# Feed-forward passes of 512 moving columns in layers 1 to 3, and smaller reorderings, in a four-layer float32 encoder trunk

## The chip, the cores and the metric

The kernel runs on one core of one Trainium2 chip. The metric is the device time of one execution in microseconds, as the median of several runs. The profile is of one further execution of the same program. TensorE is PE in its rows (its weight loads are PEld), VectorE is DVE, ScalarE is ACT, GpSimd is POOL, and SP is the queue that issues most transfers.

## What is computed

Four layers act on one sequence of 256 tokens of width 1024, in float32. Each layer has a token mixer and then a SwiGLU feed-forward of width 2816, each behind an RMSNorm and with a residual add. Layers 0 and 3 mix by attention with a forget gate, layer 1 by a diagonal state-space scan (S5), layer 2 by trailing-mean pooling.

```python
def forgetting_attention(h, w_in, b_f, w_out):
    q, k, v, f_logit = jnp.split(h @ w_in, [D_MODEL, 2 * D_MODEL, 3 * D_MODEL], axis=-1)
    log_f = jax.nn.log_sigmoid(f_logit + b_f)
    c = jnp.cumsum(log_f, axis=1).transpose(0, 2, 1)
    ...
        logits = jnp.einsum('bhqd,bhkd->bhqk', q_b, k) * scale
        logits = logits + c_b[..., :, None] - c[..., None, :]
        p = jax.nn.softmax(jnp.where(mask, logits, -jnp.inf), axis=-1)
        return jnp.einsum('bhqk,bhkd->bhqd', p, v)
    ...
    return out @ w_out

def swiglu(h, w_gate_up, w_down):
    g, u = jnp.split(h @ w_gate_up, 2, axis=-1)
    return (jax.nn.silu(g) * u) @ w_down

    for i in range(DEPTH):
        x = x + mix(rms_norm(x, mix_norm_g[i]))
        x = x + swiglu(rms_norm(x, ffn_norm_g[i]), w_gate_up[i], w_down[i])
    return rms_norm(x, final_norm_g)
```

## The kernel before

Activations lie transposed, features on the 128 partitions and the 256 tokens (`N`) along the columns. The weights come in units of 128 x 1024 float32. A unit is fetched by SP into one of four `raw` buffers; ACT then rounds it to the matmul's type (`L98`, the high part) and DVE subtracts to get the low part (`L99`), both into one of five `hl` buffers (`fetch`, `split_unit`, `unit`). Activations are split in the same way into a high and a low half, `X` in front of a projection and `H` inside the feed-forward. A product of 128 rows of the contraction is then three matmul passes of 256 columns into one PSUM bank, high by high, low by high, high by low (`term`):

```python
    def term(self, out, hl, cols, X, k, start, stop):
        self.mm(out, hl[:, 0, cols], X[:, 0, k], start, False)
        self.mm(out, hl[:, 1, cols], X[:, 0, k], False, False)
        self.mm(out, hl[:, 0, cols], X[:, 1, k], False, stop)
```

The feed-forward (`ffn`) runs 22 chunks of 128 hidden features. A chunk is two units, gate `G` and up `U`, of eight terms each, so 48 passes. `act` then takes the two banks: DVE multiplies `G` by the norm row `R` (`t`, L259), ACT applies Silu (L260), DVE multiplies with `U` (`h`, L262), ACT rounds (L178) and DVE subtracts (L179) into `H`. There are four banks with the tag `P`, two `acc` and two `tp`. The second half forms eight output tiles `d` of 22 terms each in `acc`; each is scaled by `R`, added to the residual `x` and prepared for the next norm (`settled`). A layer's feed-forward has 528 terms.

The attention (`fox`) first projects values and gates (tokens on the partitions, passes of 352, 352 and 336 columns), then `gates` computes the log-forget gate of 128 tokens at a time on ACT and DVE, PE sums it up (`sums`), DVE copies the sums out (`c`, and the transposed `nct`), and a DMA takes `nct` through memory (`nd`). `bias` on POOL reads `nd` back, spread over the partitions (`nb`), masks it and adds `c`: eight tiles of a layer, four head pairs' worth of `t` = 0 and `t` = 1. Meanwhile PE runs the q and k projections of eight head pairs, two units each. `heads` is the attention of one pair in three steps: scores on PE, then on DVE the bias and the row maximum (L402), on ACT Exp (L404), on DVE reciprocal and scaling (L407, L408); transposes of the four probability tiles on PE (L417) with copies by ACT (L419); and the product with the values, split into `oT`.

Work beside the main stream is placed by a counter: `tick` is called after a fixed number of terms (two of them in a plain projection, so four ticks a unit), and `at(n, fn)` emits `fn` n ticks later. Within a short distance the building layer may still move an instruction ahead of one that waits, so the order of each engine below is taken from the built program. Each engine executes its own list in order.

```python
            for n in (20, 25, 28):
                self.at(n, lambda steps=steps: next(steps, None))
```

Layer 0 also carries the preparation of the S5 tables (`prepare`), a long list of small DVE operations (tiles `W`, `lam`, `pa`, `pb`) that is handed out by ticks. `rstd` forms a norm row: PE sums squares (`total`), POOL raises to the power -1/2 (L228), PE spreads the row over the partitions (`spread`, L234).

Of the kernel before, what the change touches and what calls it, by code (L numbers as in the profile page):

```python
# [33 lines left out]
class Trunk:  # L34
# [128 lines left out]
    def dense(self, outs, X, ready=None):  # L163
        hls = [self.unit() for _ in outs]
        for k in range(8):
            for out, hl in zip(outs, hls):
                self.term(out, hl, slice(128 * k, 128 * k + 128), X, k, k == 0, k == 7)
                if k % 2 or len(outs) > 1 and (out is outs[1] or out is outs[-1]):
                    self.tick()

    def new_X(self, pool=None):
        return (pool or self.ap).tile([128, 2, 8, N], F32R, tag="X", name="X", bufs=1)

    def work(self, name="wk"):
        return self.ap.tile([128, N], F32, tag="wk", name=name, bufs=6)
# [5 lines left out]
    def settled(self, d, key):  # L181
# [6 lines left out]
        if key is not None and key != 2:  # L188
            g = self.gT[:, 8 * key + d:8 * key + d + 1]
            if key == 0 and d == 0:  # L190
                nc.vector.tensor_scalar(out=self.X[:, 0, d], in0=x, scalar1=g, scalar2=None, op0=ALU.mult)  # L191
            else:
                nc.scalar.activation(self.X[:, 0, d], x, AF.Identity, scale=g)  # L193
            nc.vector.scalar_tensor_tensor(out=self.X[:, 1, d], in0=x, scalar=g, in1=self.X[:, 0, d].bitcast(F32),  # L194
# [11 lines left out]
        if key is None:  # L206
            if d == 0:
                self.xg = self.ap.tile([128, 8, N], F32, tag="X", name="xg", bufs=1)
# [6 lines left out]
    def rstd(self, wait=(3, 3)):  # L215
# [34 lines left out]
    def ffn(self, l):  # L250
        nc = self.nc
        X, key = self.X, l + 1 if l + 1 < self.layers else None
        with self.tc.tile_pool(name="hidden", bufs=1, reuse_waits="tile") as hp:
            H = hp.tile([128, 2, NCH, N], F32R, name="H")
            R = self.R

            def act(i, G, U):
# [7 lines left out]
            outs = [self.bank(t)[:, 0:N] for t in ("acc", "acc", "P", "P")]  # L265
            self.dense(outs, X)
            act(0, outs[0], outs[1])
            act(1, outs[2], outs[3])
            for i in range(2, NCH):
                G, U = self.bank("P")[:, 0:N], self.bank("P")[:, 0:N]  # L270
                self.dense([G], X)
                self.dense([U], X)
                act(i, G, U)
            for d in range(8):
                o = self.bank("acc")[:, 0:N]
# [713 lines left out]
```

## Time and profile before

| | us |
|---|---|
| median of 3 runs | 1165.85 |
| lowest, highest | 1165.14, 1168.01 |
| the profiled execution | 1169.78 |
| its span (first to last instruction) | 1168.0 |
| PE busy in the span | 1133.8 |
| DVE, ACT, POOL busy | 817.0, 621.3, 130.4 |

The trace's times run from the span's start. By the stretches, layer 0's attention lies at 9 to 136 us, its feed-forward to 341; S5 at 341 to 453, feed-forward 1 to 642; pooling at 642 to 670, feed-forward 2 to 850; attention 3 at 850 to 976, feed-forward 3 to 1158. PE is busy nearly everywhere, so what counts is how many passes it runs, what one costs, and the few places where it stands. DVE is close to full only between 50 and 150 us and around 350 to 400 us. A timeline row with an xN is N instructions of one form in a row, with the time from the first start to the last end; a bracket is the idle time before the row on that engine and what ended it.

### The profile page before, as it was taken

To read this page: it belongs to the slowest core of one execution; us is meant where nothing else is said; L and a number is where in the kernel's file an instruction comes from. 1 tells how busy PE (TensorE), PEld (TensorE's weight loads), DVE (VectorE), ACT (ScalarE), POOL (GpSimd) and SP (SyncE) were. 2 spreads that over 40 slices of the span, in tenths; PEclk is the share of its full clock that TensorE was granted. 3 is DMA by queue.
4 is the path that set the end of the run, shared out by engine and by line. 5 is a ranking of instruction groups with operands and counts; after the bars stand their busy time and mean duration, and the time that the engine had idled before them with its cause. 6 is when DMAs were issued, how large, how long until landed. Compare 5 with 4: busy or idle time off the path is not lost. (4 is left out here: it accounts for less than half of the span.)

```text
span 1168.0 us, 25319 instructions
## 1 busy us (share of the span) xinstructions
PE 1133.8 (97%) x10246; PEld 1105.7 (95%) x10246; DVE 817.0 (70%) x1540; ACT 621.3 (53%) x1092; POOL 130.4 (11%) x167
## 2 busy tenths in 40 slices
PE   7899999999999999999999999999999999999996
PEld 7888899999999999999999999999999899999996
DVE  5899986888759975766555576665656767666563
ACT  5556766786852264544444554444545566444441
POOL 1287000111100000000000000000005710000000
PEclk9999999999999999999999899999999999999998
DMA  8655466788789744755566266556656644666561
GB/s 287 200 166 161 141 211 204 242 262 262 248 290 340 242 138 151 229 189 181 171 184 188 73 201 186 189 173 183 191 188 204 179 137 128 216 183 192 170 185 46
DMA packets 63285, 225.16 MB, mean 193 GB/s; under 512 B 7681, under 2 KB 8049, under 8 KB 63041
## 3 DMA queue, kind: packets, MB, share of 16 engines
q1 hardware_dynamic: 56432, 200.86, 55.0%
q0 software_dynamic: 6160, 22.00, 6.0%
q8 instruction: 80, 1.31, 0.5%
q10 hardware_dynamic: 576, 0.69, 0.2%
q14 instruction: 37, 0.30, 0.1%
HBM read 208.81 MB, written 14.71 MB: 191 GB/s over the span
## 5 line engine op out<-in xcount | busy, mean ns | idle before, releaser
L156 PE MATMUL P<-X,hl 128*128 128x256 f32 x5520 | 682.8, 284 | 2.2 <-ACT X L178 1.2
L156 PEld LDWEIGHTS P<-X,hl 128*128 128x128 f32 x5520 | 665.9, 190 | 10.8 <-issue 7.1
L98 ACT CAST hl<-raw 128x1024 fp32r<-128x1024 f32 (+3 forms) x363 | 371.7, 1027 | 394.8 <-issue 184.5
L99 DVE TENSOR_TENSOR hl<-raw,hl 128x1024 fp32r<-128x1024 f32 (+3 forms) x363 | 434.8, 1199 | 210.0 <-ACT hl L98 206.8
L156 PE MATMUL acc<-H,hl 128*128 128x256 f32 x2112 | 254.1, 281 | 0.0
L156 PEld LDWEIGHTS acc<-H,hl 128*128 128x128 f32 x2112 | 250.7, 188 | 0.8 <-issue 0.6
L156 PE MATMUL acc<-X,hl 128*128 128x256 f32 x480 | 69.4, 287 | 1.0 <-DVE u L760 0.4
L383 POOL TENSOR_SCALAR nb<-nb,c 128x128 f32<-128x128 f32 (+1 forms) x64 | 68.8, 1087 | 1.1
L156 PEld LDWEIGHTS acc<-X,hl 128*128 128x128 f32 x480 | 60.9, 188 | 3.4 <-ACT X L193 0.8
L228 POOL TENSOR_TENSOR rs<-rs,mhalf 128x2 f32<-128x2 f32 x9 | 6.5, 727 | 479.1 <-DVE rs L227 479.1
L262 DVE TENSOR_TENSOR h<-P,t 128x256 f32<-128x256 f32 x84 | 35.5, 423 | 33.6 <-PE P L156 33.4
L259 DVE TENSOR_TENSOR t<-P,R 128x256 f32<-128x256 f32 x84 | 35.5, 423 | 12.0 <-PE P L156 9.1
L404 ACT ACTIVATE pt<-pt,st 128x128 f32<-128x128 f32 (+1 forms) x64 | 28.4, 446 | 20.8 <-DVE st L402 20.7
L156 PE MATMUL P<-hl,X 128*128 128x336 f32 (+1 forms) x192 | 39.2, 324 | 0.0
L260 ACT ACTIVATE t<-t 128x256 f32<-128x256 f32 x88 | 36.4, 414 | 4.9 <-DVE t L259 4.8
L178 ACT CAST H<-h 128x256 fp32r<-128x256 f32 x88 | 35.4, 402 | 6.6 <-DVE h L262 6.6
L179 DVE TENSOR_TENSOR H<-h,H 128x256 fp32r<-128x256 f32 x88 | 36.9, 419 | 2.0 <-ACT H L178 1.9
L193 ACT ACTIVATE X<-x,gains 128x256 fp32r<-128x256 f32 x55 | 27.7, 505 | 10.8 <-DVE x L248 10.2
L202 ACT ACTIVATE s<-x 128x256 f32<-128x256 f32 x63 | 25.6, 406 | 14.4 <-DVE x L248 12.4
L156 PEld LDWEIGHTS P<-hl,X 128*128 128x128 f32 x192 | 32.7, 193 | 0.0
L156 PE MATMUL acc<-hl,X 128*128 128x352 f32 x96 | 24.6, 341 | 8.0 <-DVE X L191 7.6
L194 DVE SCALAR_TENSOR_TENSOR X<-x,gains,X 128x256 fp32r<-128x256 f32 x56 | 26.8, 480 | 5.1 <-ACT X L193 5.0
(168 smaller groups left out, 744.1 us busy)
## 6 DMA issues: line engine op xcount, KB each, us to landing
raw<-in_w_gu SPq DMA_DIRECT2D x176, 512.0 KB, 3.7
raw<-in_w_dn SPq DMA_DIRECT2D x64, 512.0 KB, 3.6
raw<-in_w_qk SPq DMA_DIRECT2D x32, 512.0 KB, 3.9
raw<-in_w_dn SPq DMA_DIRECT2D x32, 384.0 KB, 3.4
raw<-in_w_fo SPq DMA_DIRECT2D x16, 512.0 KB, 4.1
raw<-in_w_glu SPq DMA_DIRECT2D x16, 512.0 KB, 4.6
raw<-in_w_vf SPq DMA_DIRECT2D x15, 520.0 KB, 4.0
nb<-nd POOLq DMA_DIRECT2D x24, 256.0 KB, 5.2
```

Source lines behind the costliest of these rows:

```text
L98: nc.scalar.copy(hl[:, 0, s], raw[:, s])
L99: nc.vector.tensor_tensor(out=hl[:, 1, s], in0=raw[:, s], in1=hl[:, 0, s].bitcast(F32), op=ALU.subtract)
L156: self.nc.tensor.matmul(out, lhsT=lhsT, rhs=rhs, start=start, stop=stop)
L178: self.nc.scalar.copy(hi, src)
L179: self.nc.vector.tensor_tensor(out=lo, in0=src, in1=hi.bitcast(F32), op=ALU.subtract)
L193: nc.scalar.activation(self.X[:, 0, d], x, AF.Identity, scale=g)
L194: nc.vector.scalar_tensor_tensor(out=self.X[:, 1, d], in0=x, scalar=g, in1=self.X[:, 0, d].bitcast(F32), op0=ALU.mult, op1=ALU.subtract)
L259: nc.vector.tensor_tensor(out=t, in0=G, in1=R, op=ALU.mult)
L260: nc.scalar.activation(t, t, AF.Silu)
L262: nc.vector.tensor_tensor(out=h, in0=U, in1=t, op=ALU.mult)
L383: nc.gpsimd.tensor_scalar(out=nb[:, i], in0=nb[:, i], scalar1=self.c[t][:, 4 * n + i:4 * n + i + 1], scalar2=None, op0=ALU.add)
L404: nc.scalar.activation(pt, pt, AF.Exp, bias=st[:, 0:1], scale=-1.0, accum_out=st[:, 1:2])
```

## The change

1. **Wide passes.** `X` and `H` are laid out so that the high and the low half of one contraction step lie side by side (`[128, 8, 2, N]`). In the feed-forward of layers 1 to 3 a term is two passes: the high weights against both halves at once, 512 columns into a whole bank, and the low weights against the high half, 256 columns added onto the bank's second half. `fold` then adds the two halves of the bank: ACT copies the second out of PSUM, DVE adds it to the first. The last output tile (`d` = 7) of layers 1 and 3 keeps three passes. Layer 0 and all other projections keep three.
2. **Gates** of both token blocks in one set of operations, one `nct` and one `nd`, sums at tick 10 (before at 7 and 8), the first bias at 11 (before 10), the steps of `heads` at 18, 23 and 26 (before 20, 25, 28). The value copies after the first projection are in another order.
3. **Softmax scaling** of every second probability tile on ACT.
4. **Norm rows** are spread one tick later (`wait=(3, 4)`).
5. The pooling layer's second scaled band is made on ACT; S5's first two projections use `P` banks; `xg` has a buffer of its own; eight `wk` buffers.

```diff
     def term(self, out, hl, cols, X, k, start, stop):
-        self.mm(out, hl[:, 0, cols], X[:, 0, k], start, False)
-        self.mm(out, hl[:, 1, cols], X[:, 0, k], False, False)
-        self.mm(out, hl[:, 0, cols], X[:, 1, k], False, stop)
+        self.mm(out, hl[:, 0, cols], X[:, k, 0], start, False)
+        self.mm(out, hl[:, 1, cols], X[:, k, 0], False, False)
+        self.mm(out, hl[:, 0, cols], X[:, k, 1], False, stop)
...
+    def wide(self, o, hl, s, X, k, first, last):
+        self.mm(o, hl[:, 0, s], X[:, k].rearrange("p a n -> p (a n)"), first, False)
+        self.mm(o[:, N:], hl[:, 1, s], X[:, k, 0], False, last)
+
+    def fold(self, o):
+        nc = self.nc
+        lo, t = self.work("lo"), self.work("t")
+        nc.scalar.copy(lo, o[:, N:])
+        nc.vector.tensor_tensor(out=t, in0=o[:, 0:N], in1=lo, op=ALU.add)
+        return t
...
-    def rstd(self, wait=(3, 3)):
+    def rstd(self, wait=(3, 4)):
...
+            wide = l > 0
             def act(i, G, U):
-                t = self.work("t")
-                nc.vector.tensor_tensor(out=t, in0=G, in1=R, op=ALU.mult)
+                t = self.fold(G) if wide else self.work("t")
+                nc.vector.tensor_tensor(out=t, in0=t if wide else G, in1=R, op=ALU.mult)
                 nc.scalar.activation(t, t, AF.Silu)
-                h = self.work("h")
-                nc.vector.tensor_tensor(out=h, in0=U, in1=t, op=ALU.mult)
-                self.split(H[:, 0, i], H[:, 1, i], h)
+                h = self.fold(U) if wide else self.work("h")
+                nc.vector.tensor_tensor(out=h, in0=h if wide else U, in1=t, op=ALU.mult)
+                self.split(H[:, i, 0], H[:, i, 1], h)
...
+                broad = wide and not (d == 7 and key in (2, None))
+                o = self.bank("acc") if broad else self.bank("acc")[:, 0:N]
...
-            for n in (20, 25, 28):
+            for n in (18, 23, 26):
                 self.at(n, lambda steps=steps: next(steps, None))
...
-            nc.vector.tensor_copy(c, cps[:, 0:16])
-            nc.vector.tensor_copy(nct, cps[0:16, 128:256])
+            nc.vector.tensor_copy(nct, cps[0:16, 128:384])
+            nc.vector.tensor_copy(c, cps[:, 0:32])
             nc.sync.dma_start(nd, nct)
-        self.at(7 + t, sums)
+        self.at(10, sums)
...
-        for pt, st in Ps:
+        for i, (pt, st) in enumerate(Ps):
             nc.vector.reciprocal(out=st[:, 2:3], in_=st[:, 1:2])
-            nc.vector.tensor_scalar(out=pt, in0=pt, scalar1=st[:, 2:3], scalar2=None, op0=ALU.mult)
+            if i % 2:
+                nc.scalar.activation(pt, pt, AF.Identity, scale=st[:, 2:3])
+            else:
+                nc.vector.tensor_scalar(out=pt, in0=pt, scalar1=st[:, 2:3], scalar2=None, op0=ALU.mult)
...
-        nc.vector.tensor_scalar(out=sb1, in0=self.band[:, :, 144:272], scalar1=rs[:, 1:2], scalar2=None, op0=ALU.mult)
+        nc.scalar.activation(sb1, self.band[:, :, 144:272], AF.Identity, scale=rs[:, 1:2])
...
-        self.open_quad()
         for m in range(8):
             self.at(1 + 5 * m, lambda m=m: self.tables(m))
         for m in range(0, 8, 2):
-            P = [self.bank("acc")[:, 0:N] for _ in range(2)]
+            P = [self.bank("acc" if m else "P")[:, 0:N] for _ in range(2)]
             if m == 0:
                 self.dense(P, X)
+                self.open_quad()
```

Three places of the built programs follow. The number behind a name is a buffer's; `P_8953` and `P_8954` are the gate and the up bank of one chunk.

On PE, the gate and the up projection of one chunk in feed-forward 2 stood so before:

```order
L156 MATMUL P_8953<-X_8421,hl_8890 128x256 x24
L156 MATMUL P_8954<-X_8421,hl_8919 128x256 x24
```

On PE, the gate projection of a chunk of the same layer begins so now, and goes on in the same way:

```order
L156 MATMUL P_8923<-X_8052,hl_8870 128x512
L156 MATMUL P_8923<-X_8052,hl_8870 128x256
L156 MATMUL P_8923<-X_8052,hl_8870 128x512
L156 MATMUL P_8923<-X_8052,hl_8870 128x256
```

Each unit's 24 passes of 256 columns became eight pairs of 512 and 256.

On DVE, one chunk of that feed-forward before (L99 rows are weight splits; `t`, `h` and `H` are the chunk's own):

```order
L99 TENSOR_TENSOR hl_9024<-raw_8984,hl_9024 128x1024
L179 TENSOR_TENSOR H_8541<-h_8949,H_8541 128x256
L259 TENSOR_TENSOR t_9013<-P_8953,R_8537 128x256
L99 TENSOR_TENSOR hl_9053<-raw_9022,hl_9053 128x1024
L262 TENSOR_TENSOR h_9016<-P_8954,t_9013 128x256
```

On DVE, one chunk of it now:

```order
L183 TENSOR_TENSOR t_8968<-P_8923,lo_8967 128x256
L277 TENSOR_TENSOR t_8968<-t_8968,R_8168 128x256
L99 TENSOR_TENSOR hl_9005<-raw_8982,hl_9005 128x1024
L183 TENSOR_TENSOR t_8974<-P_8924,lo_8973 128x256
L280 TENSOR_TENSOR t_8974<-t_8974,t_8968 128x256
L99 TENSOR_TENSOR hl_9041<-raw_9003,hl_9041 128x1024
L194 TENSOR_TENSOR H_8172<-t_8974,H_8172 128x256
```

Two additions (L183) joined the five operations, and between any two groups of the chunk's own stands a weight split; on ACT the order is copy, weight cast, Silu, copy, weight cast, cast of `H`.

On ACT, one head pair of layer 3 before, from the last Exp on (L404 and L430 are Exp, L98 is a weight cast, L435 the scaling, L419 and L448 the copies of the transposes, L178 and L193 the cast of `oT`):

```order
L404 ACTIVATE pt_11644,st_11645<-pt_11644,st_11645 128x256
L98 CAST hl_11829<-raw_11790 128x1024
L419 COPY pT_11705<-tp_11702 128x256
L419 COPY pT_11712<-tp_11707 128x512
L98 CAST hl_11909<-raw_11827 128x1024
L178 CAST X_10986<-tp_11751 128x256
```

On ACT, one head pair of layer 3 now:

```order
L430 ACTIVATE pt_10875,st_10876<-pt_10875,st_10876 128x256
L435 ACTIVATE pt_10867<-pt_10867,st_10868 128x128
L98 CAST hl_11035<-raw_10946 128x1024
L435 ACTIVATE pt_10875<-pt_10875,st_10876 128x256
L448 COPY pT_10925<-tp_10922 128x256
L448 COPY pT_10932<-tp_10927 128x512
L98 CAST hl_11084<-raw_11033 128x1024
L193 CAST X_10233<-tp_10963 128x256
```

A weight cast now stands between the two scalings on ACT; it does so in 13 of the 16 head pairs, in the last three of layer 3 it stands behind them.

## Rows read from the trace of the kernel before

**Rows 1.** The page, part 1: span and PE's busy time, share and instructions

```profile
span 1168.0 us, 25319 instructions
PE 1133.8 (97%) x10246; PEld 1105.7 (95%) x10246; DVE 817.0 (70%) x1540; ACT 621.3 (53%) x1092; POOL 130.4 (11%) x167
```

**Rows 2.** Busy time by stretches: stretch, length, engines with counts, clock, DMA

```profile
50.00:100.00 50.00, 47.09 (x389) 43.10 (x390) 47.91 (x145) 25.86 (x60) 42.67 (x42) 0.97 0.59 172
...
750.00:800.00 50.00, 50.00 (x422) 50.00 (x422) 30.86 (x44) 23.38 (x34) 0.00 (x0) 1.00 0.58 178
```

**Rows 3.** Timeline of PE, value projection of layer 3 (start, length, instruction)

```profile
862.64 0.48 PE L156 MATMUL acc<-hl,X 128*128 128x352 f32 x2
...
871.20 0.48 PE L156 MATMUL acc<-hl,X 128*128 128x352 f32 x2
```

**Rows 4.** The page, part 5: groups, busy us and mean ns, idle before

```profile
L98 ACT CAST hl<-raw 128x1024 fp32r<-128x1024 f32 (+3 forms) x363 | 371.7, 1027 | 394.8 <-issue 184.5
L99 DVE TENSOR_TENSOR hl<-raw,hl 128x1024 fp32r<-128x1024 f32 (+3 forms) x363 | 434.8, 1199 | 210.0 <-ACT hl L98 206.8
...
L262 DVE TENSOR_TENSOR h<-P,t 128x256 f32<-128x256 f32 x84 | 35.5, 423 | 33.6 <-PE P L156 33.4
...
L260 ACT ACTIVATE t<-t 128x256 f32<-128x256 f32 x88 | 36.4, 414 | 4.9 <-DVE t L259 4.8
```

**Rows 5.** Timeline of PE where a norm row is spread

```profile
346.16 0.43 PE L234 MATMUL tp<-cst,rs 128*128 128x128 f32 x2 [0.48 <-POOL rs L228]
...
455.24 0.43 PE L234 MATMUL tp<-cst,rs 128*128 128x128 f32 x2 [0.54 <-POOL rs L228]
```

**Rows 6.** Timeline: start of S5 on PE, start of pooling on DVE

```profile
349.14 0.98 PE L156 MATMUL acc<-X,hl 128*128 128x256 f32 x6 [0.42 <-DVE u L760]
...
645.14 0.48 DVE L452 TENSOR_SCALAR sb<-band,rs 128x512 f32<-128x512 f32 x1
```

**Rows 7.** Timeline: the gate's sums on PE, copies of them on DVE

```profile
45.10 0.40 PE L156 MATMUL tp<-lf,cst 128*128 128x16 f32 x2 [1.92 <-DVE lf L356]
...
45.05 0.27 DVE L370 COPY nct<-tp 16x128 f32<-16x128 f32 x1
```

**Rows 8.** Timeline of POOL: the bias tiles of layers 0 and 3

```profile
50.05 2.59 POOL L379 DMA_DIRECT2D nb<-nd  x4 [27.13 <-DMA nd<-nct]
...
61.61 9.62 POOL L383 TENSOR_SCALAR nb<-nb,c 128x256 f32<-128x256 f32 x8
...
897.82 6.24 POOL L383 TENSOR_SCALAR nb<-nb,c 128x256 f32<-128x256 f32 x6
```

**Rows 9.** Timeline: the first head pair's softmax and transposes, layers 0 and 3

```profile
69.03 0.70 PE L417 MATMUL tp<-cst,pt 128*128 128x128 f32 x4 [0.34 <-DVE pt L408]
...
900.19 0.43 DVE L402 CUSTOM_DVE_ANT_0 pt<-acc,nb 128x256 f32<-128x256 f32 x1 [0.27 <-POOL nb L383]
...
902.41 0.44 PE L417 MATMUL tp<-cst,pt 128*128 128x128 f32 x2 [0.22 <-DVE pt L408]
```

**Rows 10.** Waits of PE, layer 0's attention: total us, times, longest

```profile
PE tp L417 <- DVE pt L408: 2.5, 4, 1.6
...
PE tp L417 <- DVE st L407: 0.8, 1, 0.8
```

**Rows 11.** Timeline of one late head pair of layer 3

```profile
956.07 0.93 PE L156 MATMUL acc<-kT,q 64*128 64x128 f32 x8
...
957.92 0.28 DVE L402 CUSTOM_DVE_ANT_0 pt<-acc,nb 128x128 f32<-128x128 f32 x1
...
959.52 0.49 ACT L404 ACTIVATE pt<-pt,st 128x256 f32<-128x256 f32 x1
...
960.05 1.05 ACT L98 CAST hl<-raw 128x1024 fp32r<-128x1024 f32 x1
...
960.57 0.82 PE L417 MATMUL tp<-cst,pt 128*128 128x128 f32 x6
```

**Rows 12.** Timeline of PE: the attention's output projection, last step

```profile
964.89 1.22 PE L156 MATMUL P<-X,hl 128*128 128x256 f32 x8 [0.60 <-ACT X L178]
```

More of the change, by code (lines that the diff above doesn't have):

```diff
@@ L253, in ffn @@
         with self.tc.tile_pool(name="hidden", bufs=1, reuse_waits="tile") as hp:
[L254 removed]
+            H = hp.tile([128, NCH, 2, N], F32R, name="H")
             R = self.R
+            wide = l > 0
+            cut = (lambda z: z) if wide else (lambda z: z[:, 0:N])
             def act(i, G, U):
[L258 to L259 removed]
+                t = self.fold(G) if wide else self.work("t")
+                nc.vector.tensor_tensor(out=t, in0=t if wide else G, in1=R, op=ALU.mult)
                 nc.scalar.activation(t, t, AF.Silu)
[L261 to L266 removed]
+                h = self.fold(U) if wide else self.work("h")
+                nc.vector.tensor_tensor(out=h, in0=h if wide else U, in1=t, op=ALU.mult)
+                self.split(H[:, i, 0], H[:, i, 1], h)
+            outs = [cut(self.bank(t)) for t in ("acc", "acc", "P", "P")]
+            self.dense(outs, X, wide)
             act(0, outs[0], outs[1])
@@ L269, in ffn @@
             for i in range(2, NCH):
-                G, U = self.bank("P")[:, 0:N], self.bank("P")[:, 0:N]
-                self.dense([G], X)
-                self.dense([U], X)
+                G, U = cut(self.bank("P")), cut(self.bank("P"))
+                self.dense([G], X, wide)
+                self.dense([U], X, wide)
                 act(i, G, U)
             for d in range(8):
-                o = self.bank("acc")[:, 0:N]
+                broad = wide and not (d == 7 and key in (2, None))
+                o = self.bank("acc") if broad else self.bank("acc")[:, 0:N]
                 for u, ks in enumerate((8, 8, 6)):
@@ L279, in ffn @@
                         f = 8 * u + k
-                        self.term(o, hl, slice(128 * k, 128 * k + 128), H, f, f == 0, f == NCH - 1)
+                        s = slice(128 * k, 128 * k + 128)
+                        (self.wide if broad else self.term)(o, hl, s, H, f, f == 0, f == NCH - 1)
                         if k % 2:
                             self.tick()
-                t = self.work("t")
-                nc.vector.tensor_tensor(out=t, in0=o, in1=R, op=ALU.mult)
+                t = self.fold(o) if broad else self.work("t")
+                nc.vector.tensor_tensor(out=t, in0=t if broad else o, in1=R, op=ALU.mult)
                 self.add(d, t)
@@ L342, in fox, with gates @@
             self.settled(d, 4 + l)
-    def gates(self, j, t, zp, r, bf):
+    def gates(self, j, zp, rs, bf):
         nc, mp = self.nc, self.mp
-        z = mp.tile([128, 4, 16], F32, tag="z", name="z", bufs=2)
-        nc.vector.scalar_tensor_tensor(out=z[:, 0], in0=zp[:, 0:16], scalar=r, in1=bf, op0=ALU.mult, op1=ALU.add)
-        lf = mp.tile([128, 16], F32, tag="lf", name="lf", bufs=2)
-        self.lf.append(lf)
+        z = mp.tile([128, 4, 32], F32, name="z")
+        for t in range(2):
+            nc.vector.scalar_tensor_tensor(out=z[:, 0, 16 * t:16 * t + 16], in0=zp[t][:, 0:16], scalar=rs[:, t:t + 1],
+                                           in1=bf, op0=ALU.mult, op1=ALU.add)
+        lf = mp.tile([128, 32], F32, name="lf")
         nc.vector.tensor_scalar(out=z[:, 1], in0=z[:, 0], scalar1=-1.0, scalar2=None, op0=ALU.mult)
@@ L857, in emit @@
         nc.scalar.activation(g.rearrange("p (j r) -> p r j", r=4), yv, AF.Gelu_apprx_tanh)
-        self.split(G[:, 0, m], G[:, 1, m], g)
+        self.split(G[:, m, 0], G[:, m, 1], g)
         self.emitted = m + 1
```

73 lines of the change are left out of this document (41 added, 32 removed).

## The prediction

> **What bounds the kernel now.** I read the page's first part, then the stretches, then the timeline at the places where PE stands. PE is busy 1133.8 of 1168.0 us [rows 1], so the time is the number of its passes times the price of one, plus a few waits. In the feed-forwards PE never stops: 50 us hold 422 passes of 256 columns [rows 2], which is 118.5 ns a pass, while DVE is busy 31 and ACT 23 of the 50. The other kind of stretch is attention in layer 0, where DVE is busy 47.9 of 50 us and PE does 389 instructions [rows 2]. There and in layer 3 PE waits for chains of small operations on other engines [rows 7, 9, 12]. So I ask of the wide passes what they take off PE, and of everything else which wait ends last.
>
> **Wide passes.** 506 of the 528 terms in layers 1 and 3 (the 22 of d = 7 stay out) and 528 in layer 2 are widened: 1540 terms. Each loses one pass and one weight load and keeps its 768 columns. A pass of 512 columns does not occur before, so its price is bounded from the nearest rows. In layer 3's value projection 54 passes of mean 346.7 columns (1040/3) lie between 862.64 and 871.20 us [rows 3], 158.5 ns each. Against 118.5 ns at 256 [rows 2] that is 40.0 ns for 90.7 columns, 0.441 ns a column, and leaves 5.6 ns for the pass itself. On this line 512 columns take 118.5 + 256 x 0.441 = 231.4 ns, and a term goes from 355.5 to 349.9 ns: 5.6 ns less. Bounds: if price is proportional to columns, 237 ns and no gain; if a column takes 1/2.4 ns (the granted clock is 1.00 of 2.4 GHz in this stretch [rows 2]) and the other 118.5 - 106.7 = 11.8 ns belong to the pass, 225.1 ns and 11.8 ns gained. I take the line, because it needs only the two widths that the trace has: 1540 x 5.6 ns = **8.6 us off**, between 0 and 18.2.
>
> The Trainium skill (TensorE: Matmul & The Clock Gate, section Back-to-back issue gap) gives N/2.4 + 2.5 ns for a warm pass in a stream, that is 109.2 ns at 256 columns. The rows show 118.5 [rows 2] and disagree by 9 ns. By that formula for both widths a term would lose just its 2.5 ns, 3.9 us in all.
>
> **What folding adds, and what hides it.** A chunk gets two ACT copies and two DVE additions of 128x256. On DVE it then has five operations of about 0.42 us [rows 4] and two weight splits of 1.2: 4.5 us. ACT has two copies, Silu and a cast at about 0.41 and two weight casts of 1.03: 3.7 us. PE needs 16 x (231.4 + 118.5) ns = 5.6 us for the chunk, so both stay under it. The waits inside the chain are covered by order: between any two steps of the chunk on DVE stands a weight split of 1.2 us, in which ACT does the 0.41 us that the next step wants. PE holds four P banks, two chunks, and five weight buffers, so one late chunk does not reach it. Cost taken: nothing; without this cover see rival 4. An output tile has 22 x 0.35 = 7.7 us of PE over some 5 us of DVE. The extra 0.8 us until x is updated falls before work that comes later: the tile d = 7 in front of pooling and the end is not folded, and in front of layer 3 the attention needs it only with its eighth unit.
>
> **Norm rows.** Four times PE stands before L234, 0.48 to 0.54 us, for POOL's power ([rows 5] has two of them, the others are at 672.7 and 978.2). One tick more is two terms in these projections, 0.7 us, which covers it: **2.0 us off**.
>
> **S5 and pooling.** The wait of 0.42 us for the eviction of an acc bank [rows 6] goes when the first two tiles use P: 0.4 off. The second band no longer queues its 0.48 us behind the first on DVE [rows 6]: 0.4 off. xg, wk and the layouts cost and bring nothing that the rows show, since PE waits for none of them.
>
> **Attention.** Here moves compete with each other, and I go by what ends last.
>
> First head pair. Scores need q and k; the softmax needs nb, which hangs on the chain gate sums, nct, nd, POOL. Before, PE stood 1.92 us for the second block's gate alone in layer 0 [rows 7], and it still had to stand again at the first transposes [rows 9]: in layer 3 DVE's fourth score tile waited for POOL and began at 900.19, and the last transposes at 902.41. So the nb chain is what ends last, and time saved ahead of it is lost in the wait for it. The change does not shorten that chain. The nct copy of both blocks comes when the second one came, one weight split (1.2 us) further down DVE's list: layer 0 before had the first nct at 45.05 and POOL's reads, freed by nd, from 50.05 [rows 7, 8]. I take +0.5 us in layer 3 (bounds 0 and 1.2) and 0 in layer 0, where POOL's operations cost 1.2 us each against 1.04 in layer 3 [rows 8] and a waiting DVE gives some back. Behind the fourth tile the last scaling now runs on ACT: 0.5 us after the tile's start Exp can begin, it and its read take 0.7 (0.49 the Exp [rows 11]), a scaling 0.4 (as Silu [rows 4]), the weight cast that stands ahead 1.05, a scaling 0.4. That ends 3.05 + 0.5 us after 900.2, about 903.7 against 902.4. And the pair starts two ticks earlier, so that 12 passes, 1.4 us, are still to do then. Layer 3: 1.3 + 1.4 = 2.7 us lost; layer 0, whose DVE was as late before, 1.4 us lost.
>
> Later pairs. Before, the scores fell on a unit's end, so the weight split released there stood ahead of the softmax: scores began at 956.07, the softmax only at 957.92, and PE's transposes followed at 960.57 without a gap [rows 11]. Two ticks earlier, the scores fall into the middle of a unit, the weight cast and split of the unit before are done, and the softmax can begin some 1.1 us earlier. ACT's last Exp then ends near 958.9, its first scaling at 959.4, the cast of 1.05 us [rows 11] at 960.4, its second scaling at 960.8; PE wants that tile four transposes (0.4 us) behind the first, at 961.0. So the extra cast is just covered: nothing gained or lost, and if the cover failed each of 13 pairs would pay (rival 3). In layer 0 PE waits at transposes for 2.5 + 0.8 us, 1.6 and 0.3 of it in the first pair [rows 9, 10]; the other 1.4 should go with 16 scalings off DVE. The last wait, 0.60 us for oT before the last step of the output projection, stands in both layers ([rows 12] has one, the other is at 136.2) and goes, since that step comes two ticks earlier: 1.2 off. Attention in sum: 2.7 + 1.4 - 1.4 - 1.2 = **1.5 us on**, with 3 us either way.
>
> **Sum.** -8.6 - 2.0 - 0.4 - 0.4 + 1.5 = -9.9 us. Against the profiled execution (1169.78, span 1168.0 and 1.8 around it) that gives 1159.9; this execution is 3.9 us above the median, and as the terms are differences I apply them to the median: 1165.85 - 9.9 = **1156 us**.
>
> **Rivals.**
> 1. *Only columns count.* A pass has no price of its own and 512 cost 237 ns. For it: 118.5 to 158.5 ns for 256 to 346.7 columns is nearly proportional (0.463 and 0.457 ns a column). Against it: the line through them still leaves 5.6 ns. Gives 1165.85 - 1.3 = 1164.6, the case too that the change does not do what it says. The Trainium skill's formula named above would give 1160.7 here.
> 2. *The surplus over the clock belongs to the pass.* 11.8 ns gained a term, 18.2 us: 1165.85 - 19.5 = 1146.4. For it: PE's clock is full [rows 2]. Against it: the surplus is larger for 346.7 columns (14.1 ns).
> 3. *The cast between the scalings shows.* If the softmax does not begin earlier, the last scaling ends 1.0 us after PE wants it, in 13 pairs: +13, so 1169, within the band of no change. For it: DVE is full in layer 0. Against it: the weight units' ends have moved, by the order of the program.
> 4. *Folding binds the feed-forward* (slower). DVE's 4.5 us a chunk fit into 5.6 only if its waits for ACT stay under 1.1. If both copies, Silu and the cast of H were all waited for, 3 x 0.41 + 0.40 us come on top: 6.2 us against 5.7 before. 66 chunks lose 33 us, the gain of 5.9 in these chunks goes, and the time is 1165.85 - 9.9 + 5.9 + 33 = 1195. It decides from 1.1 us of such waits. For it: DVE works in order and folding adds two hops. Against it: the splits between the steps, and DVE at 31 of 50 us now.
>
> **How the numbers follow.** A measurement of this kernel can tell about 0.3%, 3.5 us, from no change; faster means under 1162.4. Chances: the forecast 0.54 (own range 1151 to 1160), rival 1 0.16 (half of it above 1162.4, since 0 to 3 ns a term lie in it), rival 2 0.13, rival 3 0.09, rival 4 0.05, and 0.03 for a slower time from something unseen. Faster 0.54 + 0.13 + 0.08 = 0.75; same 0.08 + 0.09 = 0.17, slower 0.08. The range takes in the forecast, rival 1 and most of rival 2: 1145 to 1164.5.
>
> **What would show it.** In the feed-forward stretches of layers 1 to 3, 50 us should hold about 143 pairs of passes (50/0.35) with PE full; 140.6 would be rival 1, 145.5 rival 2. If PE shows idle time there that DVE ends, rival 4 holds. L234 should have no wait but in pooling and at the end. The first transposes of layers 0 and 3 should show a longer wait than before, ended by ACT's scaling, and the later ones none; waits of 1 us there would be rival 3. The gate sums should have none. I would be wrong above all if a 512-column pass costs other than 231 ns, since 1540 of them multiply the error.

## The result, and the profile after

| | before | changed |
|---|---|---|
| median of 5 runs, us | 1167.73 | 1157.62 |
| lowest, highest | 1165.14, 1169.14 | 1155.12, 1161.29 |
| span of the profiled execution | 1168.0 | 1155.8 |
| PE rows in it | 10246 | 8706 |

The ratio of the means is 0.9923, 95% interval 0.9897 to 0.995. That is 9.0 us less by the means, 10.1 by the medians and 12.2 by the two profiled spans. The forecast was 1156, worked out from a median of 1165.85 before; the five runs here have 1167.73.

The page of the changed kernel, part 1, answers to [rows 1]: 1540 passes fewer, and DVE and ACT with 52 and 62 us more.

```profile
span 1155.8 us, 22388 instructions
PE 1119.3 (97%) x8706; PEld 1027.9 (89%) x8706; DVE 868.6 (75%) x1647; ACT 683.7 (59%) x1273; POOL 121.5 (11%) x167
```

Stretches of feed-forwards 2 and 3 in the changed kernel (columns as in [rows 2], whose second row they answer to):

```profile
675.00:800.00 125.00, 125.00 (x723) 110.24 (x722) 100.52 (x160) 77.04 (x134) 0.00 (x0) 1.00 0.62 193
980.00:1090.00 110.00, 110.00 (x636) 97.00 (x635) 89.55 (x146) 68.96 (x122) 0.00 (x0) 1.00 0.61 195
```

PE never stops, DVE and ACT have room. 723 passes are 361.5 pairs: 345.8 ns a term, where 349.9 were forecast. (Both stretches lie mostly in the gate and up half of a feed-forward.)

PE's waits in the changed kernel, whole program (us in total, times, longest):

```profile
PE tp L446 <- DVE pt L437: 6.3, 3, 5.6
PE tp L249 <- POOL rs L243: 3.8, 6, 1.1
PE tp L446 <- DVE st L433: 2.4, 2, 2.0
PE tp L446 <- ACT pt L435: 2.0, 4, 0.7
PE P L156 <- DVE t L183: 2.0, 2, 1.0
PE P L156 <- ACT y L501: 1.3, 1, 1.3
```

The L446 rows are the transposes of attention, L249 the norm rows, and L183, the fold, is new: PE waits for it twice.

Lengths of stages are read below from the first pass that spreads a norm row to the last pass of that layer. Feed-forwards 1, 2 and 3 took 185.7, 177.6 and 179.3 us before and 183.5, 173.2 and 175.3 after; everything up to the end of layer 0 took 341.0 and 340.9.

### The profile page after: what moved, and what is told of

It is laid out like the page before. It is cut to its first block, busy times and chain, and to the rows that moved or that the text cites. A ratio compares the mean times of both kernels' runs of the same rounds, so it can differ in the third digit from the quotient of the medians.

```text
span 1155.8 us, 22388 instructions
## 1 busy us (share of the span) xinstructions
PE 1119.3 (97%) x8706; PEld 1027.9 (89%) x8706; DVE 868.6 (75%) x1647; ACT 683.7 (59%) x1273; POOL 121.5 (11%) x167
## 5 line engine op out<-in xcount | busy, mean ns | idle before, releaser
L156 PE MATMUL P<-X,hl 128*128 128x256 f32 (+1 forms) x4560 | 678.1, 308 | 3.4 <-DVE t L183 2.0
L156 PEld LDWEIGHTS P<-X,hl 128*128 128x128 f32 x4560 | 618.2, 190 | 52.7 <-issue 6.9
L99 DVE TENSOR_TENSOR hl<-raw,hl 128x1024 fp32r<-128x1024 f32 (+3 forms) x363 | 434.7, 1199 | 143.0 <-ACT hl L98 134.9
L98 ACT CAST hl<-raw 128x1024 fp32r<-128x1024 f32 (+3 forms) x363 | 372.3, 1028 | 162.3 <-PE acc L156 75.5
L156 PE MATMUL acc<-H,hl 128*128 128x512 f32 (+1 forms) x1628 | 251.1, 315 | 0.0
L156 PEld LDWEIGHTS acc<-H,hl 128*128 128x128 f32 x1628 | 226.6, 188 | 21.1 <-issue 0.6
L182 ACT COPY lo<-P 128x256 f32<-128x256 f32 x126 | 46.8, 372 | 107.8 <-PE P L156 107.8
L183 DVE TENSOR_TENSOR t<-P,lo 128x256 f32<-128x256 f32 x126 | 53.2, 424 | 44.4 <-ACT lo L182 44.3
L156 PE MATMUL acc<-X,hl 128*128 128x256 f32 (+1 forms) x384 | 61.3, 300 | 0.1
L156 PEld LDWEIGHTS acc<-X,hl 128*128 128x128 f32 x384 | 50.5, 188 | 3.7 <-DVE X L194 0.3
L430 ACT ACTIVATE pt<-pt,st 128x128 f32<-128x128 f32 (+1 forms) x64 | 28.6, 448 | 24.5 <-DVE st L428 24.3
L280 DVE TENSOR_TENSOR t<-t 128x256 f32<-128x256 f32 x66 | 28.0, 424 | 1.9
L277 DVE TENSOR_TENSOR t<-t,R 128x256 f32<-128x256 f32 x66 | 28.0, 424 | 1.7
```

Source lines behind the costliest of these rows:

```text
L98: nc.scalar.copy(hl[:, 0, s], raw[:, s])
L99: nc.vector.tensor_tensor(out=hl[:, 1, s], in0=raw[:, s], in1=hl[:, 0, s].bitcast(F32), op=ALU.subtract)
L156: self.nc.tensor.matmul(out, lhsT=lhsT, rhs=rhs, start=start, stop=stop)
L182: nc.scalar.copy(lo, o[:, N:])
L183: nc.vector.tensor_tensor(out=t, in0=o[:, 0:N], in1=lo, op=ALU.add)
L277: nc.vector.tensor_tensor(out=t, in0=t if wide else G, in1=R, op=ALU.mult)
```

## The experiments

All times are medians, each kernel compared with runs of the kernel before on the same chip; ratios are of the means, with their 95% interval. The kernel before had medians of 1167.86 us beside narrow, swap, spread7 and first28, 1168.52 beside nbchain, dvescale, heads20 and wide0, and 1169.57 beside before_wide, best and best_w0. So a difference of 2 us from the changed kernel's 1157.62 says little, and where two intervals overlap the rows have to decide. Unless it is said otherwise, a kernel is the changed one with the edit shown.

### Wide passes off, and alone

**narrow**

```diff
-            wide = l > 0
+            wide = False
```

> The changed kernel with three passes of 256 columns again in every feed-forward; the rest of the change stays. My theory: a wide term saves 9.6 ns (start to start 229.8 + 117.0 ns against 3 x 118.8), 1540 terms 14.8 us, of which three waits at the start of each wide feed-forward (1.2, 1.4, 1.1 us, for a bank that the fold still reads) take 3.7 back. So this kernel should take 11 us more than the changed one, 1168 to 1169 us, its 512-column rows gone, the three waits gone and 50 us of feed-forward 2 again holding some 422 passes. Rival, the line of the prediction (5.6 ns a term, 8.6 us): only 5 us more, 1162.5, and the rest of the gain would have to come from the attention and the pooling.

1168.07 us, ratio to before 0.9997 (0.9985 to 1.0009). All of the gain hangs on the wide passes, and the rest of the change is worth nothing that can be measured. The same stretches in narrow:

```profile
675.00:800.00 125.00, 125.00 (x1053) 125.00 (x1053) 79.50 (x109) 59.14 (x88) 0.00 (x0) 1.00 0.63 191
980.00:1090.00 110.00, 110.00 (x926) 110.00 (x925) 73.22 (x104) 55.59 (x83) 0.00 (x0) 1.00 0.62 194
```

1053 passes in 125 us are 356.1 ns a term, so a wide term saves 10.3 ns here. The starts of the single passes between 680 and 775 us say the same and say where: a pass of 256 columns takes 119.0 ns from its start to the next one's in narrow; in the changed kernel one of 512 takes 229.9, and the one of 256 behind it 117.0. That is 10.1 ns a term.

The price holds in the gate and up half of a feed-forward (1056 of the 1540 terms). In the half that forms the output tiles the wide terms save less: from the first pass on `H` to the last, feed-forwards 1, 2 and 3 take 64.0, 62.5 and 62.5 us in narrow and 64.1, 61.2 and 61.3 in the changed kernel, which is nothing, 7.6 and 8.1 ns a term. In feed-forward 1 transposes for the pooling stand between the output tiles. The 22 terms of one tile there, in narrow and in the changed kernel (a merged row names one of its two forms):

```profile
591.23 8.02 PE L156 MATMUL acc<-H,hl 128*128 128x256 f32 x66
```

```profile
591.51 7.91 PE L156 MATMUL acc<-H,hl 128*128 128x256 f32 x44
```

Why the passes are dearer there is open. In sum the wide passes take off some 10.7 us in the first halves and 2.5 in the second, 13.2 in all, and not 1540 times 10.3 ns.

The three feed-forwards and the pooling are together 11.6 us longer in narrow. PE's two waits for a fold take 2.0 of the 13.2 back, and 0.9 goes at the start of feed-forward 2, where PE now comes earlier to the pooling's last tiles and stands 1.3 us for `y` (L501). On the other side the pooling is 1.1 us shorter in the changed kernel's trace, where the granted clock is 0.86 over 641 to 653 us against 0.72 in narrow; swap, with the same code there, has 0.73 at the same place, so that part belongs to the execution and not to the change.

That the other parts are worth nothing does not mean that they move nothing. PE's waits in attention before, whole program, and under them those of narrow:

```profile
PE tp L156 <- DVE lf L356: 3.8, 3, 1.9
PE tp L417 <- DVE pt L408: 3.2, 6, 1.6
PE P L156 <- ACT X L178: 1.2, 2, 0.6
PE P L156 <- ACT v L314: 0.9, 2, 0.6
PE tp L417 <- DVE st L407: 0.8, 1, 0.8
```

```profile
PE tp L446 <- DVE pt L437: 6.2, 3, 5.7
PE tp L446 <- DVE st L433: 2.0, 1, 2.0
PE tp L446 <- ACT pt L435: 1.4, 3, 0.7
PE P L156 <- ACT v L326: 0.5, 1, 0.5
PE tp L156 <- DVE lf L378: 0.3, 1, 0.3
```

9.9 us against 10.4, in one execution each. The waits for the gate (`lf`) and for `oT` (L178) went, and came back at the transposes.

**before_wide** is the other half of the cut: the kernel before with the layout, the wide passes, the fold and its buffers, and nothing else.

> The kernel before with the first part of the change alone: the layout, the wide passes of layers 1 to 3, the fold, and the buffers that go with them. Theory: the wide passes are the whole gain and need none of the rest: 14.8 us off, some 2.3 us lost to the two waits for folded banks, and less than 2 in places where PE waits for a chain whatever its passes cost: 1157 to 1158, as the changed kernel. Rival: the other parts bring some us of their own that the kernel with narrow passes did not show, since something else there took them back; then this one stays above 1160.

1158.6 us, ratio 0.9907 (0.9887 to 0.9927), the time of the changed kernel. The two halves agree: alone, the wide passes give some 11 us, and the reorderings are neither needed for that nor in the way.

### The wait for the fold

**swap**

```diff
-            outs = [cut(self.bank(t)) for t in ("acc", "acc", "P", "P")]
+            outs = [cut(self.bank(t)) for t in ("P", "P", "acc", "acc")]
```

> The changed kernel, but the first two chunks of every feed-forward take their banks in the order P, P, acc, acc instead of acc, acc, P, P. Theory: the waits of 1.2, 1.4 and 1.1 us of PE before its third chunk of feed-forwards 1, 2 and 3 come from bank order: all four banks of the first two chunks are full at the same time, the folds run one after the other, and the third chunk's up or the fourth chunk's gate wants a P bank that the second of them holds. With P folded first they go: 3.7 us less, about 1154. Rival: the folding itself (ACT copy, table load, DVE add) is late whichever bank comes first; then the waits stay at 1 us or more and the time at 1157.6.

1153.74 us, ratio 0.9871 (0.9851 to 0.9891). First the wait in the changed kernel, timeline of the first chunks of feed-forward 1:

```profile
464.95 1.28 ACT L278 ACT_TABLE_LOAD   x1
466.25 0.42 ACT L278 ACTIVATE t<-t 128x256 f32<-128x256 f32 x1
466.57 0.36 ACT L182 COPY lo<-P 128x256 f32<-128x256 f32 x1
...
467.46 0.42 DVE L183 TENSOR_TENSOR t<-P,lo 128x256 f32<-128x256 f32 x1
...
468.03 2.21 PE L156 MATMUL P<-X,hl 128*128 128x512 f32 x11 [1.01 <-DVE t L183]
```

The first two chunks run together and their four banks are full at once. The second chunk's P bank is folded last, behind the first chunk's Silu and the table that ACT loads for it, and the next chunk wants that bank. In swap, PE over the same place:

```profile
458.64 11.61 PE L156 MATMUL P<-X,hl 128*128 128x512 f32 x66
```

No wait, and feed-forwards 1 and 3 are 1.3 and 1.2 us shorter. The expectation was wrong on feed-forward 2: its wait is the one for `y`, not for a fold, and it stayed, 1.1 us. So 2.5 of the 3.9 us belong to the banks. Part of the others is the first transposes of layers 0 and 3, which waited 1.1 and 1.0 us less in this trace with no edit there.

### The norm rows

**spread7**

```diff
-    def rstd(self, wait=(3, 4)):
+    def rstd(self, wait=(3, 7)):
-                self.rstd((3, 4) if l else (9, 4))
+                self.rstd((3, 7) if l else (9, 4))
```

> The changed kernel with the norm row spread seven ticks after the sum of squares instead of four (layers 1 and 3 and all feed-forwards). Theory: one tick more did not move the spread on PE in three of four places (four passes stood between sum and spread before and four, or three wide ones, after), so PE still waited 0.43 to 0.59 us there for POOL's power; from seven ticks on the spread stands 10 to 16 passes behind the sum, and the three waits go: 1.6 us less, about 1156. Rival: POOL's power starts later when there is no hurry and the wait stays.

1156.0 us, ratio 0.99 (0.9882 to 0.9917), which overlaps the changed kernel's; here the rows decide. Ahead of feed-forward 1 in the changed kernel (PE after the sum of squares, POOL's power, the spread), and then in spread7:

```profile
452.70 0.83 PE L156 MATMUL P<-X,hl 128*128 128x512 f32 x3
...
453.19 0.71 POOL L243 TENSOR_TENSOR rs<-rs,mhalf 128x2 f32<-128x2 f32 x1 [2.73 <-DVE rs L242]
...
453.96 0.43 PE L249 MATMUL tp<-cst,rs 128*128 128x128 f32 x2 [0.43 <-POOL rs L243]
```

```profile
451.55 0.94 PE L156 MATMUL P<-X,hl 128*128 128x512 f32 x4
452.32 0.85 PE L156 MATMUL acc<-X,hl 128*128 128x512 f32 x4
453.01 0.38 PE L249 MATMUL tp<-cst,rs 128*128 128x128 f32 x2
```

The places count, not the ticks. The changed kernel has three passes between sum and spread there (four of the old ones before), although the spread was asked for a tick later: the building layer moves both instructions within a short distance, and here it had moved them by more than that tick. With eight passes between, the wait is gone, and so is the one in front of the scan (0.47). Ahead of feed-forward 2 it stayed.

### The first head pair

**nbchain**

```diff
-        for i in range(4):
-            nc.gpsimd.tensor_scalar(out=nb[:, i], in0=nb[:, i], scalar1=self.c[t][:, 4 * n + i:4 * n + i + 1],
+        for u, i in [(0, 0), (0, 1), (1, 0), (1, 1), (0, 2), (0, 3), (1, 2), (1, 3)][2 * t:2 + 6 * t] if n == 0 else [(t, i) for i in range(4)]:
+            nc.gpsimd.tensor_scalar(out=self.nb[n, u][:, i], in0=self.nb[n, u][:, i], scalar2=None, op0=ALU.add,
```

> The changed kernel; only POOL's order in the first two bias tiles of each attention differs: the additions for the first head pair (two of t = 0, two of t = 1) come before those for the second. Theory: the first transposes wait for the chain gate sums, memory, POOL, and nothing else is nearly as late; two additions of 0.88 us less one that slips between, and one select of 0.63, leave the chain: the wait in layer 0 falls from 5.6 to about 4.1 us and in layer 3 from 2.0 + 0.4 to about 1, 3 us less in sum, about 1154.6. Rival: DVE or ACT are as late as POOL there; then the waits stay and the time is 1157.6.

1155.18 us, ratio 0.9879 (0.9856 to 0.9901). Layer 0 in the changed kernel, with POOL, DVE and PE:

```profile
57.34 3.54 POOL L409 TENSOR_SCALAR nb<-nb,c 128x128 f32<-128x128 f32 x4
...
62.60 7.41 POOL L409 TENSOR_SCALAR nb<-nb,c 128x256 f32<-128x256 f32 x8
...
63.56 0.43 DVE L428 CUSTOM_DVE_ANT_0 pt<-acc,nb 128x256 f32<-128x256 f32 x1 [3.52 <-POOL nb L409]
64.46 0.43 DVE L428 CUSTOM_DVE_ANT_0 pt<-acc,nb 128x256 f32<-128x256 f32 x1 [0.47 <-POOL nb L409]
...
65.92 2.00 PE L446 MATMUL tp<-cst,pt 128*128 128x128 f32 x6 [5.64 <-DVE pt L437]
```

PE's row names a DVE scaling, but that scaling stands behind two score tiles for which DVE waits for POOL's additions. PE's first transposes in nbchain, layers 0 and 3:

```profile
65.44 1.41 PE L446 MATMUL tp<-cst,pt 128*128 128x128 f32 x4 [4.24 <-DVE pt L437]
...
892.50 1.15 PE L446 MATMUL tp<-cst,pt 128*128 128x128 f32 x4 [1.47 <-DVE pt L437]
```

The wait is 1.4 us shorter in layer 0, as expected, and 0.5 shorter in layer 3 (2.0 in the changed kernel), where 1.4 was expected. These waits vary without any edit: the traces of the changed kernel, narrow, swap, spread7 and wide0, whose attention is the same, have 4.6 to 6.6 us in layer 0 and 1.0 to 2.0 in layer 3. Another measure is the time from POOL's first read of `nd` to the transposes. In layer 0 it is 13.6 us in nbchain and 14.9 to 16.7 in those five, 1.3 less than the shortest of them, so the chain through POOL is what ends last there; in layer 3 it is 13.7 against 13.4 to 14.4, and nothing is shown. The total's interval overlaps the changed kernel's.

**first28**

```diff
-            for n in (18, 23, 26):
+            for n in (18, 23, 26) if hp else (18, 28, 31):
```

> The changed kernel, but the first head pair of each attention does its transposes at tick 28 and its values at 31 instead of 23 and 26; the other pairs stay. Theory: the first transposes wait (5.6 us in layer 0, 2.0 + 0.4 in layer 3) because the bias tiles come out of a chain (gate sums, transposed copy, memory, POOL) that the change did not shorten, while PE arrives there 3 us earlier; work put in front of the wait is free. The next pair's scores and 30 passes then come first: about 3 us less in layer 0 and 2 in layer 3, 1152.5. Rival: DVE, which is full in layer 0, is what is late; then later pairs wait as much more as the first one less, and the time stays at 1156 to 1157.

1153.94 us, ratio 0.9872 (0.985 to 0.9894): 3.7 less than the changed kernel, with an interval that ends just below that kernel's. So the time was waiting time and not DVE's work. In layer 0 some of it came back in a new place: the first pair's copies of the transposes now stood on ACT behind the second pair's Exps, and PE waited 3.6 us for them ahead of the product with the values.

**heads20**

```diff
-            for n in (18, 23, 26):
+            for n in (20, 25, 28):
```

> The changed kernel with the steps of a head pair at 20, 25 and 28 again instead of 18, 23 and 26. By the prediction the earlier start is what covers the weight cast between ACT's two scalings; without it the third rival holds and about 1.0 us shows in each of 13 pairs. The first pairs have 12 passes more in front of them, 1.4 us less of wait in each layer, and the wait for oT before the last projection step, 0.8 in each layer, is back: 1157.6 + 13 - 2.8 + 1.6 = 1169. If the cast is hidden whatever the tick, 1156.4.

1156.28 us, ratio 0.9892 (0.9874 to 0.9911). The time is the second of the two that were expected, but the reason is another one: at tick 20 the order of ACT's list differs. The cast stands between the two scalings in only 6 of the 16 pairs, all in layer 0, and behind both in the other ten. ACT in a later pair of layer 3, in the changed kernel and in heads20:

```profile
901.61 0.39 ACT L435 ACTIVATE pt<-pt,st 128x128 f32<-128x128 f32 x1
901.90 1.03 ACT L98 CAST hl<-raw 128x1024 fp32r<-128x1024 f32 x1
902.84 0.51 ACT L435 ACTIVATE pt<-pt,st 128x256 f32<-128x256 f32 x1
```

```profile
900.09 0.83 ACT L435 ACTIVATE pt<-pt,st 128x128 f32<-128x128 f32 x2
900.83 1.03 ACT L98 CAST hl<-raw 128x1024 fp32r<-128x1024 f32 x1
```

PE's waits for `oT` and for ACT's scaling in heads20:

```profile
PE P L156 <- ACT X L193: 1.2, 2, 0.6
...
PE tp L446 <- ACT pt L435: 0.3, 1, 0.3
```

The wait for `oT` is back to the digit; the waits that ACT's scaling ends are 0.3 us instead of 2.0. For layer 3 this kernel tests nothing, since the cast that should have shown is no longer in between. In the six pairs of layer 0 it is hidden at tick 20 too, but for that 0.3. What answers the third rival is the changed kernel itself: the cast stands in between in 13 pairs, and PE waits for a scaling on ACT four times, 2.0 us in all and not 13. That the two ticks are what covers the cast, as the prediction reasons, is not shown, and the six pairs speak against it.

**dvescale**

```diff
-            if i % 2:
-                nc.scalar.activation(pt, pt, AF.Identity, scale=st[:, 2:3])
-            else:
+            if True:
                 nc.vector.tensor_scalar(out=pt, in0=pt, scalar1=st[:, 2:3], scalar2=None, op0=ALU.mult)
```

> The changed kernel with all four softmax scalings of a head pair on DVE again. What the step of the prediction says: in layer 3 the last scaling of the first pair no longer stands behind a weight cast of 1.05 us on ACT, some 0.9 us less there; in layer 0 sixteen scalings of 0.4 us return to a DVE that is busy 58 of 60 us, 1.4 us more; the later pairs are indifferent. Sum 0.5 us more, 1158. Rival: the scalings on ACT are what the later pairs of layer 0 wait for in the changed kernel (waits of 0.5 to 0.7 us that ACT's L435 ends, 2.0 in sum); then it is 2 us less, 1155.6.

1155.77 us, ratio 0.9889 (0.9869 to 0.9909). PE's waits at transposes sum to 7.8 us instead of 10.7, but a norm row of layer 0 waited 1.0 longer for POOL. The interval overlaps the changed kernel's, so no more can be said of the time than that scaling on ACT brings nothing. The expectation for layer 3 has a row on its side: the first transposes there waited 0.8 and 0.7 us instead of 2.0 and 0.4, and the granted clock over the next seven us (891 to 898) was 1.00 instead of 0.56.

### Layer 0, and all corrections together

**wide0** is swap with `wide = True`, so that layer 0 has two passes a term too.

> The kernel with P banks first (1153.7), and two passes a term in the feed-forward of layer 0 as well: 528 terms of 9.6 ns, 5.1 us less, 1148.7, if the fold is hidden there too. Against it: DVE is busy 148 of 190 us in that feed-forward with the preparation of the scan's tables, and 52 additions of 0.42 us make it 170 of 185. Rival: the tables or the folds come late, PE waits at chunk banks or at the start of the scan, and 5 us or more are lost again: 1154 or above.

1152.34 us, ratio 0.9858 (0.9835 to 0.9881), an interval that overlaps swap's; the rows decide. The feed-forward of layer 0 fell from 191.6 us in swap to 188.2, 3.4 of the 5.1 expected. DVE is busy 65.8 of 70 us in the middle of it (200 to 270 us), but only once, for 0.4 us, did PE wait there for a fold. So most of what is missing is not waiting: as in the other layers the output half gives less than the price of the first half, 0.6 us here for 176 terms (68.2 to 67.6 us from the first pass on `H` to the last).

**best** has swap, spread7 and nbchain, and this:

```diff
-            for n in (18, 23, 26):
+            for n in (18, 23, 26) if hp else (18, 26, 31):
```

> The changed kernel with four corrections together: P banks first in the feed-forward (2.3 us of waits), norm rows spread seven ticks after the sum (1.6), POOL's additions for the first head pair first (1.4 in layer 0, 0.6 in layer 3), and the first pair's transposes at tick 26 and its values at 31, so that 18 passes, 2.1 us, stand in front of the wait in both layers, ahead of the second pair's scores (4.2). In sum 10 us less than the changed kernel if each is worth what its wait is: 1147.5. If they cover one another, the last two first of all, 1150.

1145.63 us, ratio 0.9804 (0.9777 to 0.983). PE's first transposes in best, layers 0 and 3 (5.64 and 2.01 us in the changed kernel):

```profile
65.20 0.56 PE L446 MATMUL tp<-cst,pt 128*128 128x128 f32 x2 [2.08 <-DVE pt L437]
...
886.00 1.05 PE L446 MATMUL tp<-cst,pt 128*128 128x128 f32 x6
```

**best_w0** is best with `wide = True`.

> As the kernel with four corrections, and two passes a term in layer 0 too, which took 3.4 us off that feed-forward in the trace: 1144 if the first holds. Rival: the S5 tables' preparation is pushed behind the scan's start by 22 us more of DVE work in layer 0; then no less than the other.

1142.48 us, ratio 0.9771 (0.975 to 0.9792): 2.3% under the kernel before. That is some 15 us under the changed one by the medians, and 17 when each is taken against the kernel before that ran beside it. The S5 tables were not late: the wait at the scan's start is 0.6 us, 0.2 in best.

## Why the prediction was right, and where it was not

The total was right: 9.9 us forecast, 10.1 measured by the medians and 9.0 by the means. The mechanism of the main term was right too. That the sum agrees this closely is in part luck: the wide passes gave 4.6 us more than forecast, and waits at the start of stages, in the norm rows and in attention, which the forecast put at less or at nothing, took about as much back.

**Wide passes**, 8.6 forecast, within 0 to 18.2; 13.2 by the rows above. The mechanism held, that every pass has a price beside its columns, and the size was off. The line through two widths held as well: the 512 columns take 229.9 ns, where it gave 231.4. What was mis-sized are the passes of 256. Before, one takes 119.0 ns from start to start and not 118.5 (the 422 in 50 us [rows 2] include those that the window's ends cut), and behind a wide pass it takes 117.0, where 118.5 was kept. The wide pass, the pass behind it and the three passes before are worth 1.5 ns each time, which makes 10.1 ns a term of the 5.6, in the gate and up half. A second step was to give all 1540 terms one price; in the output half they gave 0 to 8.1 ns.

With these numbers three widths lie on one line. 119.0 at 256 and 229.9 at 512 give 0.433 ns a column and 8.1 ns for the pass itself, and at 346.7 columns 158.3, where the value projection has 158.5 [rows 3]. By this line 8.1 ns are what one pass less brings, and 2.0 come from the cheaper pass behind a wide one, whose reason is open. Each pass also has its weight load, and both went away together, so the runs do not say to which of the two the fixed price belongs. The Trainium skill (TensorE: Matmul & The Clock Gate, section Back-to-back issue gap) has a fixed 2.5 ns for a warm pass, by which a term would save 2.5; the rows show four times that. The section gives this formula for a single pass and says that in a stream of weight loads and passes both set the spacing, so the prediction's "in a stream" is not what it says there.

**Folding**, 0 forecast. Right for the bulk: PE is full in the stretches shown, and DVE is at 80% there. Wrong at the start of feed-forwards 1 and 3, some 2.5 us. The prediction costed one chunk in the steady state; the first two chunks, whose banks all fill at once and whose Silu needs a table, are another case, and "one late chunk does not reach it" does not hold for two.

**Norm rows**, -2.0 forecast. Failed: three of the four waits stayed, since the order of the program had hardly moved although the ticks had. That could have been counted in the order: passes between sum and spread, against the 1.7 us from the sum to the end of POOL's power.

**S5 and pooling**, -0.8 forecast. The wait for an acc bank [rows 6] went, and PE stood at the scan's first product instead, again for `u`. The timeline of PE there:

```profile
349.57 1.12 PE L156 MATMUL e<-u,E 32*128 32x64 f32 x32 [0.26 <-DVE u L789]
```

The wait had moved, and was 0.26 us instead of 0.42. The pooling's first product began 0.55 us after the norm row's spread in the timeline of before and 0.56 in that of after: nothing gained there, though the second band was no longer queued behind the first [rows 6].

**Attention**, +1.5 forecast. By the waits of before and of narrow it was +0.5. The parts below come from one trace of each kernel, and the same attention code differs by 3 us in layer 0 and by 1 in layer 3 from trace to trace: layer 3's loss is 0.6 to 1.8 over the five, and in layer 0 not even the sign is sure. *Layer 3's first pair:* from the first q pass to the end of the transposes 28.6 us before, 28.9 after with 12 passes (1.4) less in it: 1.7 lost, 2.7 forecast. *Layer 0's:* 35.1 and 32.7, so 0.9 gained where 1.4 lost was forecast: POOL's eight additions took 7.41 us instead of 9.62 [rows 8], and that chain is what PE waits for. *The waits for `oT`* [rows 12] went as forecast, 1.2. *Later pairs of layer 0* should have lost their 1.4 us of wait and have 2.6, of which ACT's scaling ends 1.6: the third rival's mechanism, in three pairs of one layer and at 0.3 to 0.7 us. *The value copies* were not in the prediction: the waits for `v` fell from 0.9 to 0.5 in narrow, and to nothing in the changed kernel.

One price was overlooked altogether, the clock after a wait. Stretches behind the first transposes of layer 3, before, changed and best:

```profile
901.00:908.00 7.00, 6.66 (x59) 5.47 (x58) 4.84 (x14) 3.44 (x8) 4.96 (x7) 1.00 0.53 176
```

```profile
892.00:899.00 7.00, 6.56 (x41) 5.76 (x41) 3.09 (x3) 3.12 (x6) 3.78 (x5) 0.56 0.37 123
```

```profile
892.00:908.00 16.00, 15.79 (x147) 14.03 (x144) 11.49 (x40) 11.24 (x31) 13.22 (x15) 1.00 0.59 207
```

The granted clock is 0.56 in the changed kernel's seven us, so most of them were spent at the lower level, 1.2 GHz, with 41 instructions instead of 59. Ahead of it PE had stood 2.0 us, and the transposes behind that wait were slow already: the last two took 0.69 us, where they took 0.44 before. The next 18 passes took 4.2 us, where they took 2.4 before: 1.8 us on top of the wait. In layer 0 the clock was down in both kernels, 0.81 over 67 to 76 us before and 0.62 over 65 to 74 in the changed one. best has neither the wait nor the fall in layer 3; that it is 1.9 us under its expectation may come from this, which is not shown.

**The rivals.** The first (only columns count) falls, by 10.1 ns a term. The second, 11.8 ns a term, is nearer to the 10.1 of the gate and up half than the forecast's 5.6, but its time is not reached, since the output half gives less and the folds take some back. The third falls with the changed kernel's own waits (2.0 us and not 13). The fourth, folding as the bound, falls in the bulk, and at two places of a layer's start it showed what it looks like.

## What to carry to other kernels

Where a matmul engine is full with passes of 256 columns and the same weights meet two of them, putting both moving halves side by side pays by the fixed price of a pass (here 8 to 10 ns a term in most places, and nothing in one), if the engines beside it have room for the addition of the halves. Cost the first chunk of a loop apart from the steady state: which buffers fill at the same time, and in what order they are released. Read the price of a pass from the starts of two neighbours, since a count over a window includes the passes at its ends. Before an experiment on one order is believed, look whether the rest of the order stayed: in heads20 it had not. And when several waits depend on one chain, an earlier step only moves the wait to the chain's end; look for what PE could do in front of that wait, or shorten the chain on the engine that ends it.

## What the runs showed of the hardware that was not expected

- A fall of the granted clock can follow PE's own waits: 0.56 over 7 us behind the first transposes of layer 3 when these had waited 2.0 us. With 1.0 us of wait in the same code it was 0.76 (swap), and without a wait 1.00 (best). But heads20, with 1.2 us of wait in front of the same transposes, has 1.00 (893 to 900 us), so the length of the wait alone does not decide.
- POOL's additions on 128x256 took 1.20 us each while DVE was busy 9.6 of 9.6 us (layer 0 before [rows 8]) and 0.93 in the same place of the changed kernel, with DVE busy 6.0 of 7.4 us. The DMA share fell there too, from 0.45 to 0.12; which of the two it was is not separated.
- A pass of 256 columns took 119.0 ns behind another of 256 and 117.0 behind one of 512, in the gate and up halves of feed-forwards 2 and 3.
- ACT loads a table for Silu, 1.28 us, at the start of a feed-forward, with the first chunk's chain behind it.
